# A matmul-minus-matrix kernel rewritten with its own semaphores, two matmuls per weight load and a semaphore for every transfer

## Chip, cores, metric

The kernel runs on one core of a Trainium2 chip. The metric is device time in microseconds (us) of one execution; "span" is the length of the profiled execution inside it, about 1.8 us shorter. The engines are PE (matmul; its weight loads are listed as PEld), DVE (vector), ACT (scalar), POOL (GpSimd) and SP, which only issues transfers here. Sixteen DMA engines move the data.

## The reference

```python
batch, m, k, n = 16, 512, 1024, 768
# x: batch x m x k, weight: k x n, sub_value: batch x m x n, all float32
def reference(x, weight, sub_value):
    return (np.matmul(x, weight) - sub_value).astype(np.float32)
```

The 8192 rows of x form 64 tiles of 128 rows. Input and output together are 87.03 MB.

## The kernel before

The weights stay in SBUF as fp16. Each x tile is cast to fp16 on ACT and transposed, mostly on PE with ACT copying the result back, and for seven pairs of tiles (18, 19, 24, 25, and so on) on DVE. Sixteen matmuls per tile follow, DVE subtracts, and a store leaves. All 39 transfers stand in one queue in a fixed order, several tiles at a time. A scheduler places every semaphore.

```python
TRANSFERS = [
    ('x', 0, 1), ('w', 0, 1), ('x', 1, 1), ('w', 1, 1), ('x', 2, 1), ('w', 2, 1),
    # ... kind (x, weight, sub_value, output), first tile, number of tiles
    ('s', 4, 4), ('x', 11, 5), ('s', 8, 8), ('x', 16, 8), ('x', 24, 3), ('s', 16, 8),
    # ...
    ('x', 56, 8), ('s', 56, 8), ('o', 32, 8), ('o', 40, 8), ('o', 48, 8), ('o', 56, 4),
    ('o', 60, 2), ('o', 62, 1), ('o', 63, 1),
]
# ...
    def matmuls(mi, c):                      # c = 0..3; the weights here are the x tile
        if c == 0:
            po_t[mi] = psum_o_pool.tile([P, 2, 512], F32, name="psum_o")
        for r in range(2):
            for h in range(2):               # two halves of N, the same weights
                keep(nc.tensor.matmul(
                    po_t[mi][:, h, :NS],
                    xt_t[mi][:, 2 * P * c + r : 2 * P * (c + 1) : 2],
                    w_sb[:, c, r, h * NS : (h + 1) * NS],
                    start=(c == 0 and r == 0),
                    stop=(c == n_c - 1 and r == 1),
                ))

    def finish(mi):
        # ...
        keep(nc.vector.tensor_tensor(
            out=o, in0=po_t.pop(mi)[:, :, :NS], in1=o, op=mybir.AluOpType.subtract
        ))
        issue()                              # every transfer whose buffers are now free
```

In this form each of the 1024 matmuls gets a weight load of its own (the page lists 800 and 224 loads on L177), though the two of the inner loop share their weights.

## Time and profile before

| what | before |
|---|---|
| time, median of 4 runs | 211.01 us (210.91 to 211.28) |
| span of the profiled run | 209.4 us |
| PE / DMA queue busy | 95% / 97.7% |
| PE instruction fetches in the span | 10 of 16 KB |

The busy shares, the chain, the waits and the stretches are shown and read in the prediction below. Three more lines of the page matter later: the number of instructions, the queue that fetches PE's instructions (q8: packets, MB, share of 16 engines; its packets go from 10 to 7 when PE has 540 instructions fewer, and stay at 7 when a later run gives GpSimd more), and the group of weight loads (count; busy us and mean ns; idle before).

```profile
span 209.4 us, 2967 instructions
...
q8 instruction: 10, 0.16, 0.3%
...
L177 PEld LDWEIGHTS <-xt_tile 128*128 128x128 f16 x800 | 78.2, 98 | 41.5 <-ACT xt_tile L151 1.9
```

### The profile page before, as it was taken

The page shows a single profiled execution, that of the slowest core. Times are in us where ns is not written, and L with a number is a line of the kernel's source. Part 1 is how long each engine was busy: PE and PEld are TensorE (multiplying, and loading weights), DVE is VectorE, ACT ScalarE, POOL GpSimd, SP SyncE. Part 2 cuts the span into 40 slices and gives each one's busy share as a digit, 9 for nine tenths or more (in the row PEclk, how much of TensorE's full clock was granted, in tenths as well). Part 3 has the DMA queues.
Part 4 walks back from the last instruction along what each step waited for, and adds up shares of the span by engine and source line. Part 5 has one row for each costly group of instructions (what it writes and reads, how often), then busy time and mean ns, then how long its engine had stood idle before and what let it go on. Part 6 is the DMA issues. An engine that isn't in the chain of part 4 may idle for free.

```text
span 209.4 us, 2967 instructions
## 1 busy us (share of the span) xinstructions
PE 198.4 (95%) x1249; PEld 130.4 (62%) x1249; DVE 114.1 (54%) x186; ACT 112.6 (54%) x115; POOL 0.7 (0%) x6
## 2 busy tenths in 40 slices
PE   7998789999979999999999999999999999999990
PEld 2464467676656576676666666667666766766660
DVE  0342044206149849929946965992994795332231
ACT  3555565675396183655727629355573760765410
POOL 1000000000000000000000000000000000000000
PEclk9999999999999999999999999999999999999999
DMA  6999999999999999999999999999999999999994
GB/s 221 420 426 424 424 438 439 433 443 426 391 455 415 442 427 423 454 413 432 435 421 449 423 413 444 451 418 421 418 441 440 423 437 418 426 446 427 415 383 167
DMA packets 5629, 87.22 MB, mean 417 GB/s; under 512 B 624, under 2 KB 624, under 8 KB 2032
## 3 DMA queue, kind: packets, MB, share of 16 engines
q1 hardware_dynamic: 5616, 87.03, 97.7%
q8 instruction: 10, 0.16, 0.3%
q14 instruction: 3, 0.02, 0.0%
HBM read 61.87 MB, written 25.17 MB: 416 GB/s over the span
## 4 chain that ended last, share of the span: by engine, by line
PE 68%; DMA 20%; ACT 4%; DVE 3%; SPq 1%; issue 1%
PE psum_o L177 60%; DMA x_ring<-in_x_dram 20%; PE psum_t L144 8%; ACT x_tile L135 2%; DVE xtp_tile L165 2%; ACT xt_tile L151 1%; DVE so_ring L189 1%; SPq L110 1%; SPq L122 1%; ACT x16p_tile L132 0%
## 5 line engine op out<-in xcount | busy, mean ns | idle before, releaser
L177 PE MATMUL psum_o<-w_sb,xt_tile 128*128 128x384 f16 x800 | 145.7, 326 | 1.7 <-ACT xt_tile L151 1.1
L177 PEld LDWEIGHTS <-xt_tile 128*128 128x128 f16 x800 | 78.2, 98 | 41.5 <-ACT xt_tile L151 1.9
L189 DVE TENSOR_TENSOR so_ring<-psum_o,so_ring 128x768 f32<-128x768 f32 x64 | 60.7, 957 | 61.2 <-PE psum_o L177 41.1
L151 ACT COPY xt_tile<-psum_t 128x1024 f16<-128x1024 f16 x50 | 50.6, 1012 | 75.7 <-PE psum_t L144 74.9
L165 DVE STREAM_TRANSPOSE xtp_tile<-x16p_tile 32x256 f32<-32x256 f32 x112 | 48.8, 436 | 18.9 <-ACT x16p_tile L132 17.2
L144 PE MATMUL psum_t<-ident,x_tile 128*128 128x128 f32 x200 | 52.5, 275 | 2.8 <-ACT x_tile L135 2.4
L135 ACT CAST x_tile<-x_ring 128x1024 f16<-128x1024 f32 x50 | 51.6, 1049 | 5.5 <-DMA x_ring<-in_x_dram 5.5
L177 PE MATMUL psum_o<-w_sb,xtp_tile 128*128 128x384 f16 x224 | 42.9, 326 | 0.3 <-DVE xtp_tile L165 0.3
L144 PEld LDWEIGHTS psum_t<-ident,x_tile 128*128 128x128 f32 x200 | 27.8, 142 | 16.8 <-ACT x_tile L135 4.7
L177 PEld LDWEIGHTS <-xtp_tile 128*128 128x128 f16 x224 | 21.8, 98 | 10.4 <-DVE xtp_tile L165 0.7
L132 ACT CAST x16p_tile<-x_ring 128x1024 f16<-128x1024 f32 x14 | 14.6, 1046 | 5.8 <-DMA x_ring<-in_x_dram 4.7
L205 PE MATMUL psum_o<-idle_x,idle_w 128*128 128x512 f16 x25 | 8.8, 508 | 1.3 <-DVE idle_x L200 1.3
L112 DVE CAST w_sb<-so_ring 128x768 f16<-128x768 f32 x8 | 4.1, 556 | 10.5 <-DMA so_ring<-in_weight_dram 10.5
L205 PEld LDWEIGHTS <-idle_w 128*128 128x128 f16 x25 | 3.0, 120 | 5.0 <-issue 3.2
L135 ACT ACT_TABLE_LOAD x1 | 1.3, 1283 | 0.7 <-PEq L277 0.7
L199 DVE MEMSET idle_w<- 128x64 uint32 x1 | 0.1, 112 | 0.8 <-PEq L277 0.8
masks.py:199 POOL TENSOR_SCALAR_AFFINE_SELECT ident<-ident 128x128 f32<-128x128 f32 x1 | 0.3, 292 | 0.1
L200 DVE MEMSET idle_x<- 128x256 uint32 x1 | 0.3, 272 | 0.0
masks.py:197 POOL MEMSET ident<- 128x128 f32 x1 | 0.2, 205 | 0.3 <-POOLq L277 0.3
L277 POOL MEMSET const-bfloat16-1.0<- 128x1 bf16 x1 | 0.1, 101 | 0.0
L277 POOL MEMSET const-uint8-127<- 128x1 uint8 x1 | 0.1, 101 | 0.0
L277 POOL MEMSET const-float32-0.0<- 128x1 f32 x1 | 0.1, 98 | 0.2 <-issue 0.2
(1 smaller groups left out, 0.1 us busy)
## 6 DMA issues: line engine op xcount, KB each, us to landing
so_ring<-in_sub_value_dram SPq DMA_DIRECT2D x7, 3072.0 KB, 24.2
out_dram<-so_ring SPq DMA_DIRECT2D x7, 3072.0 KB, 31.2
x_ring<-in_x_dram SPq DMA_DIRECT2D x5, 4096.0 KB, 22.3
x_ring<-in_x_dram SPq DMA_DIRECT2D x2, 2560.0 KB, 23.3
x_ring<-in_x_dram SPq DMA_DIRECT2D x3, 1536.0 KB, 19.8
so_ring<-in_weight_dram SPq DMA_DIRECT2D x4, 768.0 KB, 8.7
x_ring<-in_x_dram SPq DMA_DIRECT2D x3, 512.0 KB, 6.2
so_ring<-in_sub_value_dram SPq DMA_DIRECT2D x1, 1536.0 KB, 22.2
```

The costliest lines, as they stand in the source:

```text
L110: keep(nc.sync.dma_start(out=st, in_=w_c[at]))
L112: keep(nc.vector.tensor_copy(out=w_sb[:, at, r], in_=st[:, r]))
L122: keep(nc.sync.dma_start(out=here, in_=there))
L132: keep(nc.scalar.copy(out=x16_t["pair", first][:, mi - first], in_=x_in))
L135: keep(nc.scalar.copy(out=x16_t[mi], in_=x_in))
L144: keep(nc.tensor.transpose(ps_t[mi].bitcast(F32)[:, c * P : (c + 1) * P], x16_t[mi].bitcast(F32)[:, c * P : (c + 1) * P], ident,))
L151: keep(nc.scalar.copy(out=xt_t[mi], in_=ps_t.pop(mi)))
L165: keep(nc.vector.transpose(xt[b * Q : (b + 1) * Q, :, a * Q : (a + 1) * Q], x16[a * Q : (a + 1) * Q, :, b * Q : (b + 1) * Q],))
L177: keep(nc.tensor.matmul(po_t[mi][:, h, :NS], xt_t[mi][:, 2 * P * c + r : 2 * P * (c + 1) : 2], w_sb[:, c, r, h * NS : (h + 1) * NS], start ...
L189: keep(nc.vector.tensor_tensor(out=o, in0=po_t.pop(mi)[:, :, :NS], in1=o, op=mybir.AluOpType.subtract))
L205: keep(nc.tensor.matmul(idle_o[:, 0], idle_w, idle_x, start=True, stop=True))
L277: nc = _bacc.Bacc("TRN2", target_bir_lowering=False, num_devices=1)
```

## The change

The intent is to keep the schedule, and to drop what the scheduler adds. The whole program is put into one critical section, in which the kernel sets its own waits and counters. The two matmuls of the inner loop share one weight load, and each of the 39 transfers gets a semaphore, where before eight were used in turn. One more matmul on zeros at the start comes along (PE counts 1250 matmuls where it counted 1249).

```diff
+    ctx.enter_context(tc.tile_critical(no_gpsimd_drain=True))
 ...
+    for name in ("ident", "idle", "w", "cast", "evac", "pair", "turn", "mul", "finish"):
+        counter[name] = tc.alloc_semaphore(name)
 ...
+            sem = tc.alloc_semaphore(f"{kind}{at}")          # in issue(), one per transfer
 ...
-                keep(nc.sync.dma_start(out=here, in_=there))
+            sp.add(lambda here=here, there=there: nc.sync.dma_start(out=here, in_=there), waits, (sem, 16))
 ...
         for r in range(2):
+            weights = xt[:, 2 * P * c + r : 2 * P * (c + 1) : 2]
+            pe.add(lambda weights=weights: nc.tensor.ldweights(weights, tile_position=(0, 0)), [w for w in waits if w[0] in ready])
+            waits = [w for w in waits if w[0] not in ready]
             for h in range(2):
-                keep(nc.tensor.matmul(
+                pe.add(lambda r=r, h=h, weights=weights: loaded_matmul(   # ldweights=False
 ...
+    for t in range(n_mt):                                     # SP, at the end
+        if t == 0 or landed["o", t] is not landed["o", t - 1]:
+            nc.sync.wait_ge(landed["o", t], 16)
```

## The prediction

> **What bounds the kernel now.** I read the page first (busy shares, slices), then the chain of work that ended last in order of time, then the waits of PE and of the DMA queue's issuer, then stretches of a few microseconds at the start and the end.
>
> The page shows two resources near their limit at once:
>
> ```profile
> PE 198.4 (95%) x1249; PEld 130.4 (62%) x1249; DVE 114.1 (54%) x186; ACT 112.6 (54%) x115; POOL 0.7 (0%) x6
> ...
> DMA  6999999999999999999999999999999999999994
> ...
> q1 hardware_dynamic: 5616, 87.03, 97.7%
> ```
>
> PE is busy 95% of 209.4 us and the DMA engines 97.7%; DVE and ACT are half idle. A busy PE is not yet a full PE, so I went to the chain in order of time (start, us, what), in its middle and its end:
>
> ```profile
> 28.41 28.13 DMA x_ring<-in_x_dram
> 56.54 0.02 issue
> 56.56 1.04 ACT x16p_tile L132
> ...
> 152.41 5.85 PE psum_o L177 x36
> 158.26 0.11 PE psum_t L144
> 158.37 0.65 PE psum_o L177 x4
> 159.02 0.11 PE psum_t L144
> ...
> 199.25 5.21 PE psum_o L177 x32
> 204.46 0.02 issue
> 204.49 0.96 DVE so_ring L189
> ```
>
> The reader is to see the pitch: 36 matmuls in 5.85 us is 162.5 ns from start to start, four take 0.65 us, a transpose 0.11 us, and the next piece starts where the last one ends. From 70.70 us (the first matmul of tile 18) to 204.46 us PE never waits. That stretch can be rebuilt: tiles 18 to 63 are 46 x 16 = 736 matmuls x 162.5 ns = 119.6 us, and the 32 tiles that PE transposes meanwhile are 128 x 0.109 us = 14.0 us; 133.6 us against 133.8 us seen. Before it stands a wait for input: the x transfer for tiles 16 to 23 lands at 56.5 us, ACT casts tiles 18 and 19 by 60.4 us, and DVE needs until 70.6 us for the pair's 16 transposes between its subtractions. PE's own waits after its first matmul are short:
>
> ```profile
> PE psum_t L144 <- ACT x_tile L135: 2.4, 2, 1.4
> PE psum_o L177 <- ACT xt_tile L151: 1.1, 1, 1.1
> PE psum_o L177 <- DVE so_ring L189: 0.6, 1, 0.6
> PE psum_o L177 <- DVE xtp_tile L165: 0.3, 1, 0.3
> ```
>
> These are 4.4 us in all (total us, times, longest), all before 71 us. At 18, 22 and 27 us they follow transfers that had just landed (x for tiles 3 and 5, sub_value for tile 1); those at 57 and 70 us (1.10 + 0.34 us) follow the x transfer above. So the first third is set by when bytes land, the rest by PE's matmul pitch.
>
> The DMA side has next to no room either. Stretches (window, length, busy of PE, PEld, DVE, ACT, POOL, clock, DMA share, GB/s):
>
> ```profile
> 80.00:100.00 20.00, 20.00 (x131) 13.48 (x130) 15.27 (x28) 10.73 (x11) 0.00 (x0) 1.00 1.01 432
> 202.00:204.00 2.00, 2.00 (x15) 1.21 (x13) 0.84 (x1) 0.00 (x0) 0.00 (x0) 1.00 0.83 338
> 206.00:208.00 2.00, 0.00 (x0) 0.00 (x0) 0.00 (x0) 0.00 (x0) 0.00 (x0) 1.00 0.56 224
> ```
>
> 87.03 MB at 432 GB/s are 201.5 us, and bytes begin to move at about 2 us. The engines fall idle only after 202 us, when PE hands over the last tiles. A faster PE alone could therefore gain some 2 us at most.
>
> [...] each load lasts 98 ns inside a pitch of 162.5 ns. [...] stretches of 20 us show 425 to 434. [...] all transfers here stand in one queue, and the x transfer for tiles 3 and 4 (5.77 MB with all before it) lands at 17.28 us, when the stretches sum to 6.26 MB moved: first in, first out within about a microsecond.
>
> **The change part by part.**
>
> Weight loads: 1024 loads for 1024 matmuls become 512, so 512 x 98 ns = 50 us of PEld go, and PEld should fall from 130 to about 80 us. All of it lay beside matmuls. The path is the 162.5 ns pitch, which a load does not lengthen: saved on the path, 0 us.
>
> A semaphore for every transfer: before, eight semaphores are used in turn, so the ninth and later transfers wait until the one eight places back has landed. The issuer's waits show it:
>
> ```profile
> SPq L122 <- DMA x_ring<-in_x_dram: 11.6, 6, 6.8
> SPq L122 <- DMA so_ring<-in_weight_dram: 6.1, 4, 1.5
> SPq L120 <- DMA so_ring<-in_sub_value_dram: 2.0, 1, 2.0
> ```
>
> That is 19.7 us of waiting, nearly all in the first 15 us, and it goes. But the order of issues is the same, and the queue is never empty: by 14.8 us transfers of 17.8 MB are issued and about 5.2 MB moved. Earlier issue into a full queue moves no byte sooner: 0 us. Later issues wait for casts, subtractions or stores in both kernels.
>
> Own semaphores on the engines: order of work on each engine is the same. PE loses 32 separate waiting instructions inside the kernel, ACT gains 31 (47 against 16), DVE loses 5. PE stood waiting for nothing in the long stretch and ACT is 46% idle, with transposes two tiles ahead: 0 us, at worst 0.1 us in the first tiles. Less PE code to fetch: 565 instructions of 64 bytes (an estimate from the page's 0.16 MB of instruction traffic) are 0.04 MB, 0.1 us of the DMA engines' time.
>
> The critical section: what it adds is on the path. At entry SP counts up a semaphore, every engine waits for it and takes one more branch. In the trace the last constant is written at 0.44 us and the first instructions after one barrier and one branch start at 0.73 us; I take another such step as 0.3 us. The first transfer, at 0.74 us now, moves to about 1.0 us, and with it every landing. At exit, after the last store, SP counts up, the other engines answer, SP waits for all, then the old final barrier follows: one more round, again 0.3 us (the last bytes move before 208.0 us and the span ends at 209.4 us with two rounds and the receipt in between).
>
> Sum: 211.0 + 0.3 + 0.3 - 0.1 = 211.5 us. I take 211.4, giving a little to the first rival below.
>
> **The rivals.** (1) [...] no trace here has two matmuls on one load. (2) Landings shift. The x transfer for tiles 16 to 23 lands at 56.5 us where 22.0 MB (all up to it) at the mean rate would be there at about 54 us, so some DMA engines run behind others. A deeper early queue could change that spread. Landing earlier gains at most the 1.10 + 0.34 us of PE's waits after it: 210.0. Landing later is paid in full. (3) A separate load with a matmul that carries none is not overlapped as before, for instance because the load waits on a semaphore. With 98 ns exposed per pair this would cost 512 x 0.1 = 50 us. The program of the kernel before already holds loads and matmuls as separate instructions, and 56 of its loads wait on semaphores without harm; I give this 2%. (4) [...] entry and exit come to 1.5 us or more: 212.5.
>
> **Range and chances.** Centre 211.4. Rivals 1 and 2 together reach down to about 209.9, rival 4 with late landings up to 212.9: this is my range. Faster by over 2% means under 206.8 us, which asks for a span of about 205.2, below the 201.5 us of transfers plus start plus the last store's 3.9 us: 2%. Slower by over 2% means over 215.2 us, and only rival 3 or something unseen does that: 3%. Within 2%: 95%.
>
> **What would show it.** Right: PEld near 80 us with 512 fewer loads, PE still about 198 us, 162.5 ns per matmul in the dense stretch, DMA share 1.0 near 430 GB/s, the early issues on SP packed at about 0.45 us with no wait for landings, first transfer near 1.0 us, the x transfer for tiles 16 to 23 landing near 56.8 us, the last subtraction starting near 204.8 us. Wrong: [...] PE's waits before 71 us changed by more than 1 us (rival 2), first transfer after 1.4 us (rival 4)[...].

The sum itself is uncut: 211.0 + 0.3 + 0.3 - 0.1 = 211.5 us, taken as 211.4. The cuts take out the account of rival 1 (a second matmul on the same load follows sooner, which was to gain 0.9 us, for 210.5 us; its size came from no trace), although 0.1 us of the choice and the lower end of the range, 209.9 us, use it. The 425 to 434 are GB/s. The 64 bytes are my estimate: 0.16 MB of instruction traffic over the 2536 PE instructions (matmuls, loads, waits) of the trace.

Two of its statements were tested later. That a load does not lengthen the pitch: 36 matmuls take 5.85 us with one load for each, before, and with one for two, after. That earlier issue moves no byte sooner: with eight transfers in flight again, the landing of the x tiles 16 to 23 and that of the last store moved by 0.02 us.

## The result, and the profile after

The changed kernel took 211.66 us (median of 4 runs, 211.14 to 211.89) against 211.01 us; the ratio is 1.0025, with a 95% interval of 1.0005 to 1.0046. Ratios here are the mean time of one kernel's runs over that of the other's of the same rounds, so not quite the ratio of the medians quoted. A second set of five runs, below, gave 211.24 against 211.06. So the kernel is the same or some 0.1 to 0.3% slower. The profiles below are single runs: that of the changed kernel is its fastest (211.14 us), that of the kernel before took 211.27 us. They show how a tie comes about, and not where the 0.2 to 0.65 us between the medians lie.

The page of the changed kernel:

```profile
span 209.4 us, 2456 instructions
...
PE 198.4 (95%) x1250; PEld 80.4 (38%) x738; DVE 114.0 (54%) x186; ACT 112.9 (54%) x115; POOL 0.7 (0%) x6
...
q1 hardware_dynamic: 5616, 87.03, 97.8%
q8 instruction: 7, 0.11, 0.2%
...
L340 PEld LDWEIGHTS <-xt_b 128*128 128x128 f16 x400 | 39.2, 98 | 58.4 <-issue 52.9
```

Half the loads are gone, PEld falls from 130.4 to 80.4 us, PE's busy time does not move, and PE fetches its code 7 times where it was 10. The chain in order of time, in its middle and at its end:

```profile
100.33 5.85 PE po_b L175 x36
...
199.21 5.21 PE po_b L175 x32
...
204.45 0.96 DVE so_ring L360
```

36 matmuls still take 5.85 us, 162.5 ns each, now with one load for two. The last subtraction starts at 204.45 us, 0.04 us earlier than before. PE's waits after its first matmuls, and SP's (total us, times, longest):

```profile
PE pt_b L289 <- ACT x_b L271: 2.4, 2, 1.4
PE po_b L175 <- ACT xt_b L296: 1.5, 1, 1.5
...
PE po_b L175 <- DVE xtp_b L316: 0.3, 1, 0.3
```

```profile
SPq L252 <- ACT x_b L271: 89.7, 7, 24.7
SPq L252 <- DVE so_ring L360: 48.9, 7, 23.0
SPq L252 <- DMA out_dram<-so_ring: 47.7, 4, 24.9
```

SP no longer waits for any load to land. Its issues show the effect: of before, the first and the fifteenth, then of the changed kernel the same two (start us, us).

```profile
0.74 0.38 SPq L122 DMA_DIRECT2D x_ring<-in_x_dram  x1
...
14.77 0.33 SPq L122 DMA_DIRECT2D so_ring<-in_sub_value_dram  x1
```

```profile
0.94 0.38 SPq L252 DMA_DIRECT2D x_ring<-in_x_dram  x1
...
8.64 1.58 SPq L252 DMA_DIRECT2D so_ring<-in_sub_value_dram  x1
```

The critical section costs 0.20 us at entry, and the fifteenth transfer is issued 6 us earlier. Two stretches of the changed kernel, in the columns of the prediction, show that the supply did not become faster:

```profile
80.00:100.00 20.00, 20.00 (x131) 8.10 (x75) 15.29 (x28) 10.73 (x11) 0.00 (x0) 1.00 1.00 431
...
206.00:208.00 2.00, 0.00 (x0) 0.00 (x0) 0.00 (x0) 0.00 (x0) 0.00 (x0) 0.96 0.53 207
```

So far nothing seems to have happened. Yet the two spans of 209.4 us are made up differently at their ends. The trace has a record for every packet of every transfer. For each transfer one can read when each of the 16 DMA engines finished its part (my own reading of those records; us from the span's start):

```
                                          before    after
x tiles 16-23, slowest engine              56.09    56.13
last subtraction starts                   204.49   204.45
store of tiles 40-47, fastest engine      189.85   190.17
store of tiles 40-47, slowest engine      193.24   192.66
last store, 8th of 16 engines             207.35   207.31
last store, slowest engine                208.10   207.40
end of span                               209.4    209.4
last landing to end of span                 1.3      2.0
```

The last store is complete 0.70 us earlier, and the program then needs 0.7 us longer to end. Part of the longer end can be named. In the view of the launch line's instructions, GpSimd clears the program's semaphores (ns min/median/max, first and last start in us); before, then after:

```profile
L288 POOLq EVENT_SEMAPHORE_RANGE_CLEAR  x1: 96/96/96, 209.0 to 209.0; - x1
```

```profile
L482 POOLq EVENT_SEMAPHORE_RANGE_CLEAR  x1: 331/331/331, 208.7 to 208.7; - x1
```

As built, the range is 12 semaphores before and 54 after. That is 0.235 us of the 0.7. The rest, some 0.45 us, are the further rounds of waiting between the engines that leaving the section brings: from the last store's semaphore to the drain on SP with which the common end begins, it was 0.14 us before and is 0.58 us after.

The earlier last landing is harder. Here the fetches of PE's code come in. Each is one packet of 16 KB whose record lasts 0.97 to 1.10 us. The records do not name the engine of a packet, but the 16 finishing times of each transfer show that the distances between the engines mostly keep to some hundredths of a microsecond until a fetch comes. Then one engine falls back, and stays back as long as the queue is full: from 0.46 to 1.98 us behind the fastest after the first fetch before, from 0.65 to 2.19 us after the second, some 1.5 us each and so more than the packet lasts (why is open). By the semaphore records the slowest engine is then 1.96 to 2.32 us behind the fastest at every landing from 25 to 178 us. Before, fetches start at 22.1, 44.8, 65.3, 84.2, 103.7, 123.4, 143.2, 162.5, 182.7 and 201.6 us. After, there are seven, the last at 177.5 us. Up to the eighth fetch before, no engine is more than 2.2 us behind, so no two of the eight hit the same one. The ninth, at 182.7 us, hits one that was late already: the slowest engine finishes the store of tiles 40 to 47 3.39 us behind the fastest. In the changed kernel, by the same reckoning, no engine is hit twice, and the distance is 2.49 us. That fetches delay the end is the theory which the experiments had to test.

### The profile page after: what moved, and what is told of

Same layout as the page of the kernel before. It is cut to its first block, busy times and chain, and to the rows that moved or that the text cites. A ratio compares the mean times of both kernels' runs of the same rounds, so it can differ in the third digit from the quotient of the medians.

```text
span 209.4 us, 2456 instructions
## 1 busy us (share of the span) xinstructions
PE 198.4 (95%) x1250; PEld 80.4 (38%) x738; DVE 114.0 (54%) x186; ACT 112.9 (54%) x115; POOL 0.7 (0%) x6
## 4 chain that ended last, share of the span: by engine, by line
PE 80%; DMA 6%; DVE 5%; ACT 4%; SPq 2%; issue 1%; ACTq 0%
PE po_b L175 71%; PE pt_b L289 10%; DMA x_ring<-in_x_dram 6%; DVE xtp_b L316 3%; ACT x_b L271 2%; ACT xt_b L296 1%; DVE so_ring L360 1%; SPq L223 1%; SPq L252 1%; ACT x16p_b L271 0%; SPq L482 0%; ACTq L56 0%; SPq L129 0%
## 5 line engine op out<-in xcount | busy, mean ns | idle before, releaser
L175 PE MATMUL po_b<-w_sb,xt_b 128*128 128x384 f16 x800 | 145.7, 326 | 1.5 <-ACT xt_b L296 1.5
L360 DVE TENSOR_TENSOR so_ring<-po_b,so_ring 128x768 f32<-128x768 f32 x64 | 60.7, 956 | 60.5 <-PE po_b L175 40.2
L296 ACT COPY xt_b<-pt_b 128x1024 f16<-128x1024 f16 x50 | 50.6, 1012 | 73.8 <-PE pt_b L289 73.1
L340 PEld LDWEIGHTS <-xt_b 128*128 128x128 f16 x400 | 39.2, 98 | 58.4 <-issue 52.9
L316 DVE STREAM_TRANSPOSE xtp_b<-x16p_b 32x256 f32<-32x256 f32 x112 | 48.8, 436 | 19.3 <-ACT x16p_b L271 17.4
L289 PE MATMUL pt_b<-ident,x_b 128*128 128x128 f32 x200 | 52.3, 274 | 2.7 <-ACT x_b L271 2.4
L271 ACT CAST x_b<-x_ring 128x1024 f16<-128x1024 f32 x50 | 51.6, 1048 | 5.9 <-DMA x_ring<-in_x_dram 5.9
L289 PEld LDWEIGHTS pt_b<-ident,x_b 128*128 128x128 f32 x200 | 27.6, 141 | 46.3 <-issue 40.4
L175 PE MATMUL po_b<-w_sb,xtp_b 128*128 128x384 f16 x224 | 42.9, 326 | 0.3 <-DVE xtp_b L316 0.3
L271 ACT CAST x16p_b<-x_ring 128x1024 f16<-128x1024 f32 x14 | 14.6, 1046 | 6.8 <-DMA x_ring<-in_x_dram 6.8
```

Of the source, the lines that this page charges most:

```text
L175: return nc.tensor.add_instruction(mybir.InstMatmult(name=nc.get_next_instruction_name(), engine=full.engine, ins=list(full.ins), outs=lis ...
L271: act.add(lambda: nc.scalar.copy(out=to, in_=x_in), waits, count("cast"))
L289: pe.add(lambda: nc.tensor.transpose(words, from_, ident), waits, count("turn") if last else None)
L296: act.add(lambda: nc.scalar.copy(out=xt_b[:, d], in_=pt_b[:, b]), waits, count("evac"))
L316: dve.add(lambda: nc.vector.transpose(xt[b * Q : (b + 1) * Q, :, a * Q : (a + 1) * Q], x16[a * Q : (a + 1) * Q, :, b * Q : (b + 1) * Q],), ...
L340: pe.add(lambda weights=weights: nc.tensor.ldweights(weights, tile_position=(0, 0)), [w for w in waits if w[0] in ready])
```

## The experiments

Twelve kernels ran on three chips. The kernel before took 211.06 us (11 runs), 211.17 us (11) and 211.07 us (9) there. The prediction's own account (T1) says that halving the loads gains nothing on the path and the section costs the difference. The rival (F) says that the halved loads do gain, by fewer instruction fetches on the DMA engines, and that the section's cost at entry and exit eats the gain. Its premise is that a transfer counts as landed only with its slowest engine. The trace shows that here. Before, the semaphore records of the last store run from 207.61 us (the first of 16 engines) to 208.51 us (the last), and SP, which waits for it, goes on at 208.53 us. Those of the x tiles 16 to 23 run from 54.37 to 56.54 us, and the first cast of these tiles starts at 56.56 us. (The table above goes by packets: 208.10 and 56.09 us for the slowest engine of the two, some 0.4 us before its semaphore record.)

### The changed kernel once more

No edit.

> The changed kernel once more, unaltered, as the measure for the three runs beside it. Theory T1 (the loads and the eight-deep queue are worth nothing; entry and exit of the critical section cost about 0.20 us at the start and 0.5 to 0.75 us at the end): 211.5 to 211.9 us against 211.0 of the kernel before, ratio 1.002 to 1.004. Theory T2 (the 0.65 us of the first measurement was drift of single runs): ratio 0.999 to 1.001.

Measured: 211.24 us (211.07 to 211.52, 5 runs), ratio to before 1.0011 (0.9994 to 1.0027). In its profile the last store landed at 207.49 us, with a span of 209.5 us. This is the yardstick for its three companions.

### One load for each matmul again

```diff
-            pe.add(lambda weights=weights: nc.tensor.ldweights(weights, ...
-            waits = [w for w in waits if w[0] not in ready]
             for h in range(2):
+                pe.add(lambda weights=weights: nc.tensor.ldweights(weights, ...
+                waits = [w for w in waits if w[0] not in ready]
```

> Undoes the weight-load half alone: a load before each of the 1024 matmuls again, inside the critical section. T1: within 0.2 us of the changed kernel in the same call, weight-load busy time back from 80 to about 130 us, matmul pitch 162.5 ns in both. Rival (the halved loads do gain, and the section costs more than the net shows): slower than the changed kernel by 0.5 to 1.3 us.

Measured: 212.24 us (211.92 to 212.8, 6 runs), ratio 1.0059 (1.0042 to 1.0077), so 1.0 us more than with halved loads on the same chip, and the two ranges do not touch. The page and the end of the chain:

```profile
PE 198.4 (94%) x1250; PEld 130.3 (62%) x1250; DVE 114.1 (54%) x186; ACT 112.8 (54%) x115; POOL 0.7 (0%) x6
```

```profile
199.56 5.21 PE po_b L175 x32
...
204.80 0.96 DVE so_ring L360
```

PEld is back at 130 us, yet 32 matmuls take 5.21 us as they do with shared loads. So T1 was right on the pitch and wrong on the sum: the halved loads are worth about a microsecond that does not come from the pitch. There are nine PE fetches where there were seven (the companion's eighth, at 209.22 us, comes after its last store); 512 instructions of 64 bytes (the estimate of the prediction) are 32 KB, just two of them. The slowest engine is 3.21 us behind the fastest at the store of tiles 40 to 47 (2.46 us in its companion), and the last store lands at 208.20 us, against 207.49 us. In the span this is 0.7 us of the microsecond. Of it 0.26 us are already in the last subtraction (204.80 against 204.54 us), of which a later landing of the x tiles 16 to 23 (56.39 against 56.22 us) can explain 0.17 us. The other 0.45 us are one late DMA engine at the last store: 15 of the 16 are done by 207.74 us.

### Eight transfers in flight at most

```diff
+    def eight():
+        return [(in_order[-9], 16)] if len(in_order) > 8 else []
 ...
-            sp.add(lambda ...: nc.sync.dma_start(out=here, in_=there), waits, (sem, 16))
+            sp.add(lambda ...: nc.sync.dma_start(out=here, in_=there), eight() + waits, (sem, 16))
```

> Undoes the semaphore per transfer in its effect: each transfer is issued only after the one eight places ahead of it has landed. T1: within 0.2 us of the changed kernel; the sync engine's waits on landings return (some 20 us in the first 15 us), and no landing moves by more than 0.5 us because the queue stays full. Rival (a deeper queue shifts landings): the x transfer for tiles 16 to 23 lands over 0.5 us earlier or later than the changed kernel's 56.6 us, and the time follows.

Measured: 211.63 us (211.14 to 212.31, 6 runs), ratio 1.0029 (1.0007 to 1.005). SP's waits on the landings of loads are back; the two largest are these:

```profile
SPq L257 <- DMA so_ring<-in_weight_dram: 6.0, 4, 1.6
SPq L56 <- DMA x_ring<-in_x_dram: 2.2, 1, 2.2
```

The fifteenth transfer is issued at 14.95 us, but the x tiles 16 to 23 land at 56.20 us and the last store at 207.47 us, both within 0.02 us of the unaltered run's. The medians differ by 0.39 us with overlapping intervals and no later landing, so I read it as no effect that these runs can show. A semaphore for every transfer moved issues and not bytes.

### A second critical section

```diff
+    with tc.tile_critical(no_gpsimd_drain=True):
+        first = tc.alloc_semaphore("first")
+        with nc.sbuf_tensor("first_b", [P, 8], F32) as first_b:
+            nc.vector.memset(first_b.ap(), 0.0).then_inc(first, 1)
+            for engine in (nc.sync, nc.tensor, nc.scalar, nc.gpsimd):
+                engine.wait_ge(first, 1)
+
     ctx.enter_context(tc.tile_critical(no_gpsimd_drain=True))
```

> Doubles the suspected cost: a second critical section, all but empty (one tiny write on the vector engine that the other engines wait for), before the real one. T1: one more entry (0.2 us), one more exit round (0.4 to 0.5 us) [...]: 0.6 to 1.0 us over the changed kernel, all of it seen as a later first transfer (1.6 to 1.9 us in place of 0.94 us). Rival T2: within 0.2 us of the changed kernel.

Measured: 212.56 us (212.35 to 212.84, 6 runs), ratio 1.007 (1.0053 to 1.0087), 1.3 us more than with one section and more than I expected. (The 0.6 to 1.0 us expected held an allowance for the handshake; entry and exit alone are 0.6 to 0.7 us.) The first transfer is issued at 2.06 us, 1.12 us later; the last store lands 1.00 us later than in the first run. So what delays the first transfer is paid nearly in full at the end, with 0.79 us of it in the last subtraction (205.33 us). A PE fetch at 202.34 us, as late as the last one before, leaves the slowest engine only 0.3 us behind the median at the last store (PE ends later here, too): a late fetch does not have to cost its full size.

### Fetches on the idle engine, first design

```diff
+    for k in range(1, 63):
+        for _ in range(80):
+            pool.add(lambda k=k: nc.gpsimd.wait_ge(counter["mul"], k))
```

> The changed kernel with some 2,480 extra instructions on the idle GpSimd engine: waits for counts that PE has reached or reaches anyway, spread over the tiles. No engine that works gets an instruction more; only the fetches of instructions grow, by about ten of 16 KB. Theory F (each fetch holds one of the 16 DMA engines for about 1 us, a transfer lands with its slowest engine, and so the halved weight loads gained by two fetches fewer): 0.5 to 2 us slower than the changed kernel (211.24 in the last call, ratio 1.001), the x transfer for tiles 16 to 23 landing after 56.7 us, the spread of the 16 engines at one landing wider. Rival (the extra weight loads of the earlier run cost PE or SBUF time, not DMA time): within 0.2 us of the changed kernel.

Measured: 335.56 us, ratio 1.59. The design failed. (As built, two waits become one instruction: the trace has 2486 waiting instructions on GpSimd against 6. So 80 a tile in the edit are 40 instructions, and 34 in the second design are 17.) GpSimd should only have been given code to fetch, with waits that PE's counter meets in time. It could not keep up, and SP stood 121.7 us at the end waiting for it. The time says nothing on F. The trace says a little: the last subtraction started at 204.61 us as usual, but the last store landed at 209.66 us.

### More semaphores, none of them used

```diff
+    spare = [tc.alloc_semaphore(f"spare{n}") for n in range(96)]
```

> The changed kernel with 96 more semaphores allocated and never used. The clearing of semaphores at the end took 96 ns for a range of 12 (before) and 331 ns for a range of 54 (changed), 5.6 ns each. Theory: it takes 331 + 96 x 5.6 = 870 ns, and the time grows by about 0.5 us. Rival (the clearing lies beside other work at the end): the same time within 0.2 us.

Measured: 212.01 us (211.82 to 212.62, 6 runs), ratio 1.0046 (1.0034 to 1.0058). The clearing:

```profile
L483 POOLq EVENT_SEMAPHORE_RANGE_CLEAR  x1: 851/851/851, 208.9 to 208.9; - x1
```

96 more semaphores cost 520 ns, 5.4 ns each. The last store had landed at 207.31 us and the span ended at 210.1 us, 2.7 us later (2.0 in the changed kernel). Of the 0.77 us between them the clearing makes up 0.52, and GpSimd's drain just before it another 0.14 (268 ns in place of 128). The clearing is on the path.

### The x transfer for tiles 16 to 23 in two halves, in both kernels

The same edit in the changed kernel, then in the kernel before. It lets tiles 18 and 19 start earlier, and so moves PE's work away from the end.

```diff
-    ('s', 4, 4), ('x', 11, 5), ('s', 8, 8), ('x', 16, 8), ('x', 24, 3), ('s', 16, 8),
+    ('s', 4, 4), ('x', 11, 5), ('s', 8, 8), ('x', 16, 4), ('x', 20, 4), ('x', 24, 3), ('s', 16, 8),
```

> The changed kernel with the x transfer for tiles 16 to 23 cut into two of four tiles. The first lands some 5 us earlier (2.1 MB at 430 GB/s), PE's last two waits (1.5 to 1.7 us and 0.3 us) vanish, and PE ends at about 202.7 us instead of 204.4. Theory (two bounds at once): the stores at the end are then held by the DMA engines, where the last one can land at about 206.5 us instead of 207.4, so 0.6 to 0.9 us faster than the changed kernel. Rival (PE alone is the bound): 1.7 us faster.

> The same cut in the kernel before. PE's waits of 1.10 and 0.34 us vanish and PE ends 1.4 us earlier. Its last landing is already held by one DMA engine that took an instruction fetch at 201.6 us (208.10 us against 207.4 in the changed kernel), so theory F says 0 to 0.4 us faster than the kernel before; PE as the only bound says 1.4 us.

Measured: 211.19 us (210.7 to 212.25, 6 runs), ratio 1.0005 (0.9987 to 1.0023), and 211.18 us (211.03 to 211.49, 5 runs), ratio 1.0002 (0.999 to 1.0014). The chains end like this, changed kernel first:

```profile
196.83 5.21 PE po_b L175 x32
...
202.06 0.96 DVE so_ring L360
```

```profile
202.32 0.96 DVE so_ring L189
```

PE is done over 2 us earlier in both, and neither kernel gains more than the noise: the DMA engines hold the end. With PE out of the way in both, the fetches show best here, though the two kernels differ in more than these. The last store lands at 208.03 us with ten PE fetches and at 207.00 us with seven, a gain of 1.03 us. The slower exit and entry of the changed kernel use it up, and the times are equal.

### Fetches on the idle engine, second design

```diff
+    for k in range(1, 63):
+        for _ in range(34):
+            pool.add(lambda k=k: nc.gpsimd.wait_ge(counter["mul"], k))
```

> The earlier run with extra waits on GpSimd ended 122 us late because GpSimd itself could not keep up (134 ns for each of 40 waits a tile); but its last store landed at 209.66 us where the changed kernel's lands at 207.40, with PE ending at the same time. Here 17 waits a tile, 2.3 us of the 3.0 us that PE takes, so GpSimd keeps up and only about eight fetches of 8 KB are added. Theory F (a fetch holds one DMA engine and the last store lands with the slowest engine): PE's last subtraction starts at 204.4 to 204.7 us as in the changed kernel, the last landing comes 0.3 to 1.5 us after 207.4, and the time is 0.3 to 1.5 us above the changed kernel's 211.24 to 211.66. Rival: within 0.2 us.

Measured: 213.69 us (213.58 to 213.77, 4 runs), ratio 1.012 (1.0105 to 1.0135), 2.0 to 2.4 us above the changed kernel's medians and more than I expected. GpSimd kept up this time: SP never waits for it at the end. Its fetches appear in q14, apart from PE's q8; q14 has 3 packets in the changed kernel, where GpSimd is idle. PE ends no later than without them: the last subtraction starts at 204.26 us.

```profile
q14 instruction: 11, 0.09, 0.1%
```

Eight more packets of 8 KB, each taking about 0.31 us, so 0.1% of the DMA engines' time, made the last store land at 209.85 us instead of 207.40 us. The median engine finished it at 207.16 us, as early as ever. Only the slowest ones are late: the distance from the fastest to the slowest engine grows from 2.34 us at the landing at 146.4 us to 4.52 us at the store of tiles 40 to 47, where the changed kernel goes from 2.28 to 2.49 us. The direction is what F says. For the size, the finishing times help again: after the fetches at 166.1, 177.1 and 188.7 us the slowest engine falls from 2.59 to 3.28, 4.04 and 4.52 us behind the fastest, while at these transfers no other is more than 2.70 us behind. So several of the added fetches hit the same engine, and each set it back by 0.5 to 0.8 us, more than the 0.31 us of its packet.

### Fewer bytes

Wrong on purpose (relative error 0.71): sub_value is not loaded for tiles 32 to 63, 12.6 MB less.

```diff
+            if kind == "s" and at >= NSO:
+                for t in span:
+                    landed["s", t] = landed["o", t - NSO]
+                continue
             sem = tc.alloc_semaphore(f"{kind}{at}")
```

> Wrong on purpose: the sub_value of tiles 32 to 63 is not loaded (12.6 MB, 29 us of the DMA engines' time); the subtraction takes what the ring holds, after its store has landed. Theory (PE's matmul pitch and the DMA engines bind together, and the changed kernel's end is the last subtraction plus a store): PE ends at 204.4 us as before, the last store lands at about 207.3 us, time 0 to 0.3 us below the changed kernel. Rival (DMA alone binds): over 5 us faster.

Measured: 211.63 us (211.08 to 212.44, 4 runs), ratio 1.003 (1.0001 to 1.0059). The DMA engines stand still for whole stretches, one of them this (the columns as above):

```profile
115.00:120.00 5.00, 5.00 (x34) 1.95 (x19) 4.84 (x10) 2.98 (x4) 0.00 (x0) 1.00 0.00 0
```

PE works on through it, the last subtraction starts at 204.47 us and the last store lands at 207.41 us. Bytes alone do not set the end: PE holds it too.

### Fewer matmuls

Wrong on purpose (relative error 0.29): 88 of the 1024 matmuls left out, 88 x 162.5 ns = 14.3 us of PE.

```diff
+                if mi >= 20 and c in (1, 2) and r == 0 and h == 1:
+                    continue
                 pe.add(lambda r=r, h=h, weights=weights: loaded_matmul(
```

> Wrong on purpose: from tile 20 on two of sixteen matmuls of each tile are left out, 88 x 162.5 ns = 14.3 us of PE. Theory (both bind): the transfers, which keep their number, end with their engines, as in the run with the x transfer cut in two, at about 206.5 to 207.0 us, so 0.3 to 1.0 us faster than the changed kernel and no more. Rival (PE alone binds): 10 us or more faster.

Measured: 211.01 us (210.75 to 211.25, 4 runs), ratio 0.9993 (0.9976 to 1.001). PE's busy time falls by 11.9 us in the page (from 198.4; the 14.3 us were an estimate from the pitch), the last subtraction starts at 200.26 us, 4.2 us earlier, and the last store still lands at 206.99 us. Matmuls alone do not set the end either.

```profile
PE 186.5 (89%) x1162; PEld 80.7 (39%) x738; DVE 113.4 (54%) x186; ACT 112.1 (54%) x115; POOL 0.7 (0%) x6
```

Together these runs give the two bounds. Where no engine is late, the last store lands 2.95 us after the last subtraction starts (2.94 in the run with fewer bytes). By that, an estimate for the kernel before, PE alone allows 207.44 us before and 207.40 us after. With PE out of the way, as in the runs with the x transfer cut, the DMA engines allow 208.03 us before and 207.00 us after. So the kernel before is held by its late DMA engine, and the changed one by PE, and of the 1.03 us that the DMA side gained only 0.70 us could be had.

### The cut, with eight semaphores in turn

The cut transfer of the earlier run, and eight semaphores for all transfers in place of 39, to shorten the clearing.

```diff
-    ('s', 4, 4), ('x', 11, 5), ('s', 8, 8), ('x', 16, 8), ('x', 24, 3), ('s', 16, 8),
+    ('s', 4, 4), ('x', 11, 5), ('s', 8, 8), ('x', 16, 4), ('x', 20, 4), ('x', 24, 3), ('s', 16, 8),
 ...
+    eight = [tc.alloc_semaphore(f"moved{n}") for n in range(8)]
 ...
-            sem = tc.alloc_semaphore(f"{kind}{at}")
+            sem, full, free = turn()          # the next of the eight, its value, the wait for its last use
```

> A candidate for better than both: the changed kernel with the x transfer cut in two and with eight semaphores taken in turn for the transfers, so that the range cleared at the end falls from 54 to 22 or so. Theory: 0.17 us less clearing than the run with the cut alone (ratio 1.0005 to the kernel before), so a ratio of 0.999 to 1.000; not better than the kernel before beyond noise, because the DMA engines hold the end.

Measured: 211.12 us (210.87 to 211.44, 5 runs), ratio 1.000 (0.9985 to 1.0015). The clearing fell from 331 to 161 ns. This was the best candidate that I had, and it only equals the kernel before.

## Why the prediction was right or wrong

The time was right (211.4 predicted, 211.66 and 211.24 measured), and so was the reading that PE and the DMA engines bind at once. Cutting PE's busy time by 11.9 us gained at most 0.7 us against the changed kernel, cutting 12.6 MB gained nothing, and moving PE's end over 2 us forward gained nothing in either kernel (I had allowed "some 2 us at most"). By its own steps:

- **Weight loads, "saved on the path, 0 us".** Right for the matmul pitch: 36 matmuls take 5.85 us in both kernels, so the pitch changes in neither direction, and rivals 1 and 3 are out. As a value of the halved loads it was wrong: undoing it alone costs 1.0 us.
- **"Less PE code to fetch ... 0.1 us of the DMA engines' time".** This is the step that failed. The bytes were about right (36 KB estimated, three fetches of 16 KB seen; the trace counts 540 fewer PE instructions, not 565), but I spread them over 16 engines. Each fetch sets one engine back by some 1.5 us, and the last store waits for the slowest. With PE out of the way the last store landed 1.03 us earlier with seven fetches than with ten; in the two kernels compared here it was 0.70 us. The changed kernel's landing repeats: 207.31 to 207.49 us in four profiles with seven fetches before it (its own two, eight in flight, spare semaphores).
- **A semaphore for every transfer, 0 us.** Right. The issues moved by 6 us, the landing of the x tiles 16 to 23 by 0.04 us, and going back to eight in flight moved that landing and the last store's by 0.02 us. Rival 2 did not come about. PE's wait of 0.6 us behind a subtraction went, but it is back (0.7 us) in the run with a load for each matmul, which keeps the deep queue. That x landing does show how some engines run behind, as I had guessed: the two slowest, 1.98 and 2.19 us behind the fastest before, are those that had taken the first two fetches; the next is 0.82 us behind.
- **Own semaphores, 0 us.** Nothing speaks against it: PE never waits in the long stretch in either kernel. It was not tested alone.
- **Entry, 0.3 us.** Measured 0.20 us for the first transfer: the trace has SP's count at 0.72 us, a branch on each engine at 0.76 to 0.82 us, and the transfer at 0.94 us. I expected every landing to move with it and the last subtraction to start near 204.8 us. It started at 204.45 us, and the slowest engine's landing of the x tiles 16 to 23 moved by 0.04 us although the median engine's moved by 0.48 us (54.20 to 54.68). Both kernels had taken two PE fetches by then. The engine that the second one hit had been 0.65 us behind before and 0.48 us after, and that makes up for the 0.19 us by which the fastest engine is later. So the delay was absorbed by luck, and the run with two sections shows what a later start costs otherwise.
- **Exit, 0.3 us.** The mechanism was right: the trace has SP's count at 207.98 us, the other engines' answers at 208.02 us, SP's last wait for them at 208.28 us, and SP joining the final barrier at 208.39 us. The size was not: 0.7 us. I had left out the clearing of 42 more semaphores, 0.235 us, whose price the run with 96 spare ones confirms; the waiting rounds make up some 0.45 us, where I had 0.3. With the entry this is 0.9 us, between my 0.6 and the 1.5 of rival 4.

So the sum came out by luck, by two errors that cancel: a gain of 0.7 us that I had put at 0.1, and an exit of 0.7 us that I had put at 0.3, with the entry's delay absorbed on the way. One sum of the range was wrong, too: by their own terms (0.9 us is that of rival 1) rivals 1 and 2 together reach down to 211.4 - 0.9 - 1.4 = 209.1 us, not 209.9. That the change "does nothing" is true of the total only.

Still open: No run changed the fetches and nothing else. Undoing the shared loads changes PE's instructions too, and the added waits on GpSimd read semaphores besides being fetched; what speaks for the fetches is that engines fall back when a fetch comes, and that both runs leave PE's pitch alone and delay the slowest engine far more than the median one (median at the last store 207.66 us with a load for each matmul against 207.40 us in its companion, and 207.16 us with the added waits). Which fetch makes the late engine at the last store is not shown: before has one at 201.6 us, but in the run with a load for each matmul the last comes at 183.94 us. Open is also what a shared load would do in the scheduled kernel, where a load is added before every matmul as it is built (1249 loads for 1249 matmuls in the page). A form of the changed kernel with PE's stream in a loop was not run, so what it does to the fetches is not shown.

## What to carry to other kernels

Where the DMA engines are full, as they are here, count instruction fetches by what they do to a single engine (1.5 us each for PE's), and look at the slowest of the 16 in every landing, since that one is waited for (here SP went on at 208.53 us, 0.02 us after the last of 16 semaphore records and 0.92 us after the first). Where two resources end within some microseconds of each other, take work off each alone before hoping for a gain from either. A section with semaphores of its own paid 0.2 us at entry and 0.7 us at exit here, and every semaphore in its range took 5.4 ns to clear at the end, on the path.
